# Holding TensorE's products to the order in which the program emits them

## The chip, the cores and the metric

The kernel runs on one core of a Trainium2 chip. The metric is the device time of one execution in microseconds (us), lower is better. A run's figure is the median of several executions.

## The reference

A block of four sequence mixers over 2048 tokens of 1024 features, depth 1, all in fp32:

```python
h = _rmsnorm(x, pre_norm_w)
proj = einsum('btd,de->bte', h, w_in)          # 1024 -> 3984 columns
p_gdn, p_rwkv, p_sc, p_gla = _split(proj, [1032, 1152, 1024, 784])
y = concatenate([_gated_deltanet(p_gdn), _rwkv7(p_rwkv), _short_conv(p_sc), _gla(p_gla)])
out = einsum('bte,ed->btd', y, w_out)
x = x + _rmsnorm(out, post_norm_w)
```

Gated DeltaNet, RWKV-7 and GLA are recurrences over time with 4 heads each. The kernel computes them in chunks of 64 tokens: inside a chunk with small matrix products, and for the first two with the inverse of a triangular 64x64 matrix; from chunk to chunk a state is carried. The short convolution has no state beyond two tokens.

## The kernel before, in words

**The large products.** Time is cut into four blocks of 512 tokens. For each block the input projection is computed in 31 tiles of 128 columns and one narrow tile (called "x" in the code). An fp32 product is made of three fp32r products (high times high, high times low, low times high), so that a tile takes 24 products of 128x128 by 512, in groups of 4: 760 of them in a block (method `proj`, line 476). They accumulate in the PSUM tile `pp`, of which there are two. The output projection (`out_proj`, line 1345) has the same form: 16 time tiles by 48 products.

**The small products.** All else on TensorE is small: transposes (`psa`, by `tr`), chunk matrices (`psa<-AR,BK`, `psa<-kq`), the inverses (`inverse`, line 558: twelve steps, each a handful of products into `psi` followed by VectorE work on the result) and the chains that carry the states (`psc`: `gdn_chain`, `rwkv_chain`, `gla`). Each step of an inverse or a chain needs the step before it, through VectorE or ScalarE.

**The order of emission.** Every kind of work is a Python generator, a "thread" with a priority: the chains 0, the inverses 1, the preparation of matrices 2, output of finished tiles 3, statistics and the scaled input of the next block 4, loading of the output weights 5, and 99 for the main thread, the projections. `weave` (line 227) decides what is emitted next by a clock of its own, `self.t`, that `mm` and `tr` advance by an estimate of each product's time (a group of four large products counts 0.86 us). The main thread emits one group at a time. When at least `BEAT = 2.3` us of that clock have gone by since the last visit, that is after three groups or 12 large products, and some other thread is ready, all ready threads are stepped until none is ready: a visit. A thread that yields a number is ready again that much later; the numbers stand in the table `LAT` (0.48 to 8 us). A thread that yields a tuple waits until that event has been declared by `done`, plus its `lat`. If the main thread itself waits for an event, the visits follow each other with no large products between them, and the clock jumps ahead where nobody is ready.

Three such waits of the main thread matter here:

- `projections` (line 1394) puts ("R", blk - 1) before the first RWKV tile of a block (line 1404), because the tiles that hold the last block's RWKV operands are used again. The event comes from `put` (line 1196): 8.0 us after the last RWKV chain step of the last block its result is transposed (`psa<-cst,or`, two products a time tile), and 3.0 us after that ("R", blk - 1) holds (line 1203).
- `proj` waits for "F", pieces of the scaled input of the next block (`hh` and `hl`, method `front`, line 405).
- `out_proj` begins with `yield "W", 0` (line 1347). `load_out` (line 1333) starts to load the output weights when ("G", 3) holds, 3.0 us after the last DeltaNet transposes (`psa<-cst,og`), and steps eight times with 2.8 us (`LAT["wo0"]`); the event comes 2.0 us later.

**The compiled order.** The program is then scheduled at compile time. The scheduler takes each engine's instructions in the order of emission as long as they are ready by its own model of times; where the next one isn't, it lets a later one that is ready go first, on TensorE as on the others. Some instructions stand in `high_priority` blocks and go ahead; no product is among them. TensorE then runs its products in the compiled order, and waits where one's input is late.

Of the kernel before, what the change touches and what calls it, by code (L numbers as in the profile page):

```python
# [125 lines left out]
class Ring:  # L126


    def __init__(self, pool, name, shape, dtype, n):
        self.t = [pool.tile(shape, dtype, name=f"{name}{i}", tag=f"{name}{i}") for i in range(n)]  # L130
        self.i = 0
# [56 lines left out]
class K:  # L188
    def __init__(self, tc, a, out):
        self.tc, self.nc, self.a, self.out = tc, tc.nc, a, out  # L190
        self.t, self.left, self.ev, self.threads = 0.0, 0.0, {}, []


    def mm(self, out, w, x, **kw):
        n = math.prod(out.shape[1:])
        self.t += max(0.028, n * (1.67e-3 if w.dtype == F32 else 0.42e-3))
        return self.nc.tensor.matmul(out, w, x, **kw)  # L197

    def tr(self, out, x, ident):
        self.t += out.shape[1] * 0.83e-3  # L200
        return self.nc.tensor.transpose(out, x, ident)  # L201

    def thread(self, gen, prio):
        self.threads.append([prio, 0.0, None, gen])
# [1253 lines left out]
```

## Time and profile before

| what | value |
|---|---|
| median of three runs | 1382.74 us (1379.66 to 1382.91) |
| the profiled execution | 1378.93 us |
| its span in the trace | 1377.1 us |
| mean granted TensorE clock | 0.986 |
| TensorE (PE) busy | 1287.9 us, 94% |
| VectorE (DVE) busy | 973.3 us, 71% |
| ScalarE (ACT), GpSimd (POOL) busy | 530.4 us, 360.3 us |

The span is the time from the first to the last instruction in the trace; 1.8 us of the execution lie around it. All durations below are from this one execution. PE rows in the trace have modelled ends, so the time a group of products takes is best read as the distance from its start to the start of what follows it on PE. An fp32 product stands as two rows of the hardware (x16 is eight products in the code); fp32r, fp16 products and transposes stand as one.

### The profile page before, as it was taken

The numbers are of one execution on the slowest core, as the hardware profiler recorded it, in microseconds if no ns is written. First come the engines' busy times: TensorE is split into PE (matmuls) and PEld (weight loads), VectorE is DVE, ScalarE is ACT, GpSimd is POOL, SyncE is SP. The second block draws the span as 40 slices with busy tenths as digits, with TensorE's granted clock in tenths as the row PEclk, the third lists the DMA queues.
The fourth block names the chain that finished last, engine by engine and source line by source line (L and its number), as shares of the span: only waits on it lengthen the run. The fifth ranks groups of instructions, "written<-read, shape, count | busy, mean of one in ns | idle before, by whom it ended". The sixth has DMA issues, their size and how long they took to land. (4 is left out here: it accounts for less than half of the span.)

```text
span 1377.1 us, 25663 instructions
## 1 busy us (share of the span) xinstructions
PE 1287.9 (94%) x9928; PEld 978.6 (71%) x9928; DVE 973.3 (71%) x2194; ACT 530.4 (39%) x1181; POOL 360.3 (26%) x437
## 2 busy tenths in 40 slices
PE   5979987899999999999999899999999998999997
PEld 3767765677777767777677677676776775677886
DVE  4767489989874897687847985878659948744322
ACT  4654345344532341335423523353225325232221
POOL 5555454311121121111301210103112126223221
PEclk9999999999999999999999999999999998999999
DMA  7876653444344324554344344442443344333442
GB/s 262 281 257 218 238 179 127 156 135 141 127 134 151 126 99 150 159 156 136 124 152 136 104 140 160 144 134 72 140 159 112 129 143 138 102 100 119 151 148 100
DMA packets 98507, 204.48 MB, mean 148 GB/s; under 512 B 9152, under 2 KB 39248, under 8 KB 98384
## 3 DMA queue, kind: packets, MB, share of 16 engines
q1 hardware_dynamic: 98384, 202.83, 44.9%
q8 instruction: 78, 1.28, 0.4%
q14 instruction: 45, 0.37, 0.1%
HBM read 153.51 MB, written 49.28 MB: 147 GB/s over the span
## 5 line engine op out<-in xcount | busy, mean ns | idle before, releaser
L197 PE MATMUL pp<-hh,w 128*128 128x512 f32 (+1 forms) x2272 | 646.6, 407 | 8.7 <-ACT hh L432 5.2
L197 PEld LDWEIGHTS pp<-hh,w 128*128 128x128 f32 (+1 forms) x2272 | 415.0, 190 | 99.9 <-ACT hh L432 4.8
L197 PE MATMUL pp<-hl,w 128*128 128x512 f32 (+1 forms) x1152 | 339.5, 405 | 2.2 <-POOL hl L433 2.0
L197 PEld LDWEIGHTS pp<-hl,w 128*128 128x128 f32 (+1 forms) x1152 | 208.2, 188 | 48.4 <-POOL hl L433 3.8
L350 POOL TENSOR_TENSOR w<-raw,w 128x512 fp32r<-128x512 f32 (+1 forms) x102 | 131.2, 1288 | 212.8 <-ACT w L349 120.1
L349 ACT CAST w<-raw 128x512 fp32r<-128x512 f32 (+1 forms) x102 | 60.3, 593 | 146.4 <-PE pp L197 74.8
L354 POOL TENSOR_TENSOR sm<-sm,mhalf 128x4 f32<-128x4 f32 (+1 forms) x64 | 58.6, 915 | 213.0 <-DVE sm L1091 185.5
L197 PE MATMUL pp<-woh,w 128*128 128x512 f32 x256 | 73.2, 402 | 1.1 <-ACT w L349 1.1
L659 DVE SCALAR_TENSOR_TENSOR pq<-pq,par,pq 128x512 f32<-128x512 f32 x72 | 58.9, 817 | 15.3 <-ACT pq L656 10.4
L583 DVE COPY Yb<-Y 64x512 f16<-64x512 f16 x160 | 63.5, 397 | 1.8
L833 ACT COPY pq<-pp 128x512 f32<-128x512 f32 x36 | 21.1, 587 | 97.7 <-PE pp L197 97.7
L197 PEld LDWEIGHTS pp<-woh,w 128*128 128x128 f32 x256 | 47.5, 190 | 10.7 <-ACT w L349 1.5
L1030 DVE TENSOR_TENSOR Sg<-Sg,psc 64x128 f32<-64x128 f32 x64 | 18.1, 283 | 46.9 <-PE psc L197 46.1
L596 DVE TENSOR_TENSOR X<-psi,X 128x512 f16<-128x512 f32 x64 | 43.9, 686 | 8.7 <-PE psi L197 8.2
L197 PEld LDWEIGHTS <-Bb 128*128 128x128 f16 x768 | 29.7, 99 | 28.5 <-issue 19.9
L197 PEld LDWEIGHTS <-Yb 128*128 128x128 f16 x640 | 25.4, 99 | 33.5 <-issue 23.3
L197 PE MATMUL psi<-X,Bb 128*128 128x64 f16 x768 | 39.3, 195 | 9.7 <-DVE X L579 7.0
L197 PE MATMUL psi<-W,Yb 128*128 128x64 f16 x640 | 33.0, 195 | 15.5 <-DVE W L591 12.7
L1391 DVE SCALAR_TENSOR_TENSOR pq<-pq,sm,x 128x512 f32<-128x512 f32 x32 | 24.5, 765 | 30.3 <-DMA x<-in_x 20.4
L598 DVE STREAM_TRANSPOSE Y<-X 128x512 f16<-128x512 f16 x64 | 45.1, 704 | 0.5
L591 DVE TENSOR_TENSOR W<-psi,c 128x512 f16<-128x512 f32 x64 | 43.8, 685 | 2.0 <-PE psi L197 0.7
L1380 ACT ACTIVATE x<-pp 128x512 f32<-128x512 f32 x32 | 19.1, 597 | 55.8 <-PE pp L197 55.8
(317 smaller groups left out, 2101.1 us busy)
## 6 DMA issues: line engine op xcount, KB each, us to landing
w<-parts SPq DMA_DIRECT2D x186, 512.0 KB, 3.3
parts<-w SPq DMA_DIRECT2D x62, 512.0 KB, 4.0
raw<-in_wt SPq DMA_DIRECT2D x62, 256.0 KB, 3.1
x<-in_x SPq DMA_DIRECT2D x56, 256.0 KB, 3.0
raw<-yd SPq DMA_DIRECT2D x32, 256.0 KB, 2.9
out<-pq SPq DMA_DIRECT2D x32, 256.0 KB, 2.1
x<-in_xt SPq DMA_DIRECT2D x24, 256.0 KB, 2.7
yd<-y SPq DMA_DIRECT2D x48, 128.0 KB, 1.8
```

Source lines behind the costliest of these rows:

```text
L197: return self.nc.tensor.matmul(out, w, x, **kw)
L349: self.nc.scalar.copy(hi, src)
L350: self.nc.gpsimd.tensor_tensor(lo, src, hi.bitcast(F32), ALU.subtract)
L354: self.nc.gpsimd.tensor_tensor(dst, x, self.mhalf[:, 0:x.shape[1]], ALU.pow)
L583: nc.vector.tensor_copy(Yb[hs(c), :, hs(c)], Y[hs(c)])
L591: nc.vector.tensor_tensor(W, v(ps), m4(self.lev[lv]), ALU.mult)
L596: nc.vector.tensor_tensor(X2, v(ps), X, ALU.add)
L598: nc.vector.transpose(Y, X)
L659: nc.vector.scalar_tensor_tensor(acc, p[:, i:i + BL], self.pcol("conv", 4 * ct + i), acc, ALU.mult, ALU.add)
L833: nc.scalar.copy(p[:, 1:], ps)
L1380: nc.scalar.activation(junk, ps[i], AF.Square, accum_out=ss[:, i:i + 1])
L1391: nc.vector.scalar_tensor_tensor(o, o, r, x, ALU.mult, ALU.add)
```

## The change

Every product and transpose is given an order-only dependency on the one emitted before it. The scheduler thus has to keep TensorE's instructions in the order of emission. No semaphore comes with it; nothing else is edited, `BEAT` and `LAT` included. The orders of the other engines are still the scheduler's.

```diff
     def mm(self, out, w, x, **kw):
         n = math.prod(out.shape[1:])
         self.t += max(0.028, n * (1.67e-3 if w.dtype == F32 else 0.42e-3))
-        return self.nc.tensor.matmul(out, w, x, **kw)
+        return self.after(self.nc.tensor.matmul(out, w, x, **kw))
 
     def tr(self, out, x, ident):
         self.t += out.shape[1] * 0.83e-3
-        return self.nc.tensor.transpose(out, x, ident)
+        return self.after(self.nc.tensor.transpose(out, x, ident))
+
+    def after(self, ins):
+
+        if self.prev is not None:
+            info = mybir.DependencyInfo(mybir.DependencyClass.NoSync, mybir.DependencyReason.DATA)
+            self.tc.add_manual_dep(ins.ins, self.prev.ins.name, info, reason="order of emission")
+        self.prev = ins
+        return ins
```

## Rows read from the trace of the kernel before

**Rows 1.** The page, part 1: busy us (share of the span) xinstructions.
```profile
PE 1287.9 (94%) x9928; PEld 978.6 (71%) x9928; DVE 973.3 (71%) x2194; ACT 530.4 (39%) x1181; POOL 360.3 (26%) x437
```
**Rows 2.** Busy time by stretch; columns: stretch, its us, PE, PEld, DVE, ACT, POOL, clock, DMA.
```profile
418.84:704.82 285.98, 274.81 (x2296) 207.49 (x2291) 219.26 (x520) 111.27 (x254) 48.29 (x74) 0.99 0.43 138
...
684.80:728.00 43.20, 43.20 (x342) 33.75 (x341) 21.27 (x48) 11.51 (x25) 4.29 (x13) 1.00 0.49 156
757.50:806.70 49.20, 44.27 (x344) 33.40 (x342) 46.50 (x99) 21.67 (x48) 10.86 (x10) 0.97 0.32 105
847.90:888.00 40.10, 36.56 (x294) 26.74 (x294) 34.87 (x79) 17.25 (x39) 6.63 (x10) 1.00 0.48 153
...
645.65:664.80 19.15, 18.56 (x169) 12.28 (x167) 16.11 (x56) 11.72 (x33) 6.05 (x8) 1.00 0.51 159
```
**Rows 3.** Timeline of PE, an undisturbed stretch; columns: start, us, instruction.
```profile
684.77 1.17 PE L197 MATMUL pp<-hh,w 128*128 128x512 f32 x4
685.78 1.08 PE L197 MATMUL pp<-hl,w 128*128 128x512 f32 x4
686.70 1.08 PE L197 MATMUL pp<-hh,w 128*128 128x512 f32 x4
687.71 0.65 PE L197 MATMUL psa<-qbd,lqk 128*64 128x256 f32 x4
```
**Rows 4.** Timeline 645 to 670 us, first RWKV tile of block 2: PE, DVE, ACT.
```profile
645.65 1.19 PE L197 MATMUL pp<-hh,w 128*128 128x512 f32 x4
...
652.10 0.73 PE L197 MATMUL pp<-hh,w 128*128 128x512 f32 x2
652.67 0.27 PE L201 MATMUL psa<-cst,lg 128*128 128x128 f32 x1
...
659.68 0.42 DVE L1095 TENSOR_TENSOR or<-or,sm 128x256 f32<-128x256 f32 x1 [0.90 <-POOL sm L354]
...
662.11 0.59 ACT L833 COPY pq<-pp 128x512 f32<-128x512 f32 x1
...
663.45 1.05 PE L197 MATMUL pp<-hh,w 128*128 128x512 f32 x3
...
664.80 0.44 PE L201 MATMUL psa<-cst,or 128*128 128x128 f32 x2
...
669.94 0.39 PE L197 MATMUL psi<-X,Bb 128*128 128x64 f16 x8 [1.96 <-DVE X L579]
```
**Rows 5.** Timeline 757 to 807 us, preparation of RWKV matrices in block 2.
```profile
757.52 1.18 PE L197 MATMUL pp<-hh,w 128*128 128x512 f32 x4
...
763.59 0.39 PE L197 MATMUL psi<-W,Yb 128*128 128x64 f16 x8 [1.94 <-DVE W L591]
...
805.48 0.70 PE L197 MATMUL pp<-hh,w 128*128 128x512 f32 x2
```
**Rows 6.** Timeline: last DeltaNet transposes, and the output projection's first products.
```profile
1129.85 0.44 PE L201 MATMUL psa<-cst,og 128*128 128x128 f32 x2
...
1149.20 1.22 PE L197 MATMUL pp<-woh,w 128*128 128x512 f32 x2 [1.09 <-ACT w L349]
...
1153.98 0.66 PE L201 MATMUL psa<-cst,or 128*128 128x128 f32 x2
...
1157.14 0.52 PE L197 MATMUL pp<-woh,w 128*128 128x512 f32 x1
```
**Rows 7.** Busy time by stretch around it, columns as in rows 2.
```profile
1140.20:1147.00 6.80, 4.46 (x76) 3.85 (x76) 5.22 (x10) 5.47 (x14) 4.73 (x4) 1.00 0.51 146
1147.00:1157.20 10.20, 7.69 (x29) 4.73 (x29) 9.33 (x18) 5.56 (x14) 6.51 (x6) 0.50 0.44 125
```
**Rows 8.** Timeline of PE at the start: the first large products.
```profile
14.71 1.94 PE L197 MATMUL pp<-hh,w 128*64 128x512 f32 x4 [1.58 <-ACT hh L432]
16.45 2.13 PE L197 MATMUL pp<-hl,w 128*64 128x512 f32 x4
```

## How the change should move the time

> **What bounds the kernel.** I read the engines' busy time first: TensorE is busy 94% of the span, VectorE 71% [rows 1], so TensorE is the bound and only 89 us of it are idle. Then the busy time by stretch [rows 2]. One period of the program (418.84 to 704.82) has 11 us of TensorE idle time. In 684.8 to 728 TensorE has no gap at all; the gaps lie where VectorE is nearly full (757.5 to 806.7: 46.50 of 49.20 us) or where it and the chains are (847.9 to 888.0). Then the timeline of TensorE against the rule of emission. In the undisturbed stretch the large products come in twelves, as `weave` emits them [rows 3]: three groups, 0.92 us apart, 0.23 us a product, and 0.18 us more for the change between kinds (2.94 us in all). There the compiled order already is that of emission and the change does nothing. Elsewhere the twelves are broken: in 757.5 to 806.7 the timeline has 108 large products in 21 pieces instead of 9 (from the first to the last row of [rows 5]), and in 645.65 to 664.80 28 products in 11 pieces [rows 4]. A piece costs about 0.12 us beside its products (two products took 0.57 us from 652.10 to 652.67, against 0.46). These places are what the change edits, and the question is what each held place waits for.
>
> **The change, part by part.** It adds no instruction and no semaphore; on TensorE a product that isn't ready now holds back all that was emitted behind it.
>
> *First RWKV tile of a block, three times (blocks 1 to 3).* The code lets the main thread emit this tile only after ("R", blk - 1), that is after the last transposes `psa<-cst,or` of the block before. In the trace the tile's 24 products start at 645.65 and are evicted at 662.11, and 28 large products are done before those transposes run at 664.80 [rows 4]. The scheduler pulled all of them forward, into the waits of RWKV's and GLA's chains. Held, nothing large is there to fill in. Worked out: the transposes' input is ready at 660.10 (659.68 + 0.42), so they run 4.7 us earlier than before; behind them come the 28 products, 28 x 0.23 = 6.4 us and 0.4 us for three visits. Net 6.8 - 4.7 = +2.1 us. The event comes 3.0 us of the emission's clock later still, so some steps of the chain and the inverse run bare; the nearest row is the step at 669.94 that waits 1.96 us, and I take half of one more such wait, +1.0. The clock: after the one place where TensorE ran small products alone (1140.2 to 1147.0, busy 4.46 of 6.80 us) the granted clock was 0.50, 1.2 GHz, for the next 10.2 us [rows 7], whereas 645.65 to 664.80 kept 1.00 [rows 2]. Held, this stretch becomes like the other. I let the first eight large products run at half clock: four took 1.74 us at the start, 0.435 each [rows 8], 0.2 more than 0.23, +1.6. Fewer pieces in what follows give back some six changes, -0.7. Together +4.0, three times +12. Bounds for each: -1 (chain steps come sooner by what TensorE's large products delay them now, and the clock stays), +9 (6.8 us not covered at all, a full wait of 1.96 and no gain of pieces).
>
> By the Trainium skill, page "TensorE: Matmul & The Clock Gate", section "Part 4: PE-mode transpose", transposes do not count as activity for the clock in the way products do. With it the held stretches, rich in transposes, would run at the lower clock throughout, which is the second rival below.
>
> *Start of the output projection, once.* The main thread waits for "W", 0. The last DeltaNet transposes ran at 1129.85 [rows 6]; the event is 3.0 + 8 x 2.8 + 2.0 = 27.4 us later on the emission's clock, which while the main thread waits I take to run like real time: 1157.3. Before, the first product ran at 1149.20, and nine had run by 1157.3 (counted from 1149.20 to 1157.14 [rows 6]), at half clock [rows 7]. Held, nine products move behind, 9 x 0.23 = 2.1 us, and eight of those after the wait meet the half clock, +1.6; at the density of [rows 4], eight changes saved in 19.15 us, the next 35 us save 15, -1.7 (an estimate). Sum +2. Bounds -2 (chains and inverse, alone on TensorE, finish sooner) and +8.1 (1157.3 - 1149.2).
>
> *Preparation of RWKV matrices, four times (757.5 to 806.7).* The inverse's step at 763.59 was passed by five products more than the twelve, and still waited 1.94 us for VectorE [rows 5]. Held, TensorE waits 5 x 0.23 = 1.15 us longer there, but the products come after, while VectorE, which is busy 46.50 of 49.20 us and keeps its work, sets the pace. Twelve pieces fewer are worth 1.4 us. I take +0.5 each, +2. Bounds each: -2.7 (VectorE without a gap) and, taking the same 2.7 us once more as lost, +2.7.
>
> *The next block's first tile, three times (847.9 to 888.0).* TensorE waits 3.5 us there now, VectorE is busy 34.87 of 40.10. The tile waits for the same `hh` in either order; and pieces saved and chain steps held back behind it are of like size. 0, bounds -2 and +2 each.
>
> *Start.* The first tile's products, now taken as the pieces of `hh` come (14.71 on, at half clock), stand in pairs in the emission; one product waits for its neighbour, +0.5 [rows 8].
>
> The other engines' orders are set by priorities that the edit leaves alone: the waits that it adds delay evictions of `pp` and so the next tiles' products, both counted above as products moved. Loads of weights move with their products and are waited for nowhere in these rows except at 1149.20.
>
> Sum: 12 + 2 + 2 + 0 + 0.5 = +16.5 us on the profiled execution's 1378.93 us: 1395.4. The runs shown lie 1 to 4 us above that execution (median 1382.74), so I say **1397 us**, about 1% slower. What can be told from no change here is 0.3%, 4 us.
>
> **Rivals.** *Faster: the emission knows better than the scheduler.* The table of latencies is in the kernel's own terms, and where it fits the chip, held products wait no longer than now and the pieces vanish. Price: 8 changes saved in 645.65 to 664.80, 12 in 757.5 to 806.7 and as many in 847.9 to 888.0 (an estimate from the former), 32 x 0.12 = 3.8 us a block, 15 us in four; time about 1366. It decides if each RWKV wait costs less than 4 us, what a block saves. For it: TensorE gaps of only 11 us a block would remain even so. Against it: the three waits above are in the code, and the trace shows 28 products that passed each. Chance 0.20.
>
> *Much slower: the held stretches lose the clock.* In the three RWKV stretches TensorE is granted half its clock throughout, like 1147.0 to 1157.2. There the two transposes took 0.66 us against 0.44 [rows 4, 6]; the 12 us of small products of such a stretch (18.56 busy less 6.4) become 18: +6 each, +18 in all, 1415. For it: [rows 7]. Against: those products wait on VectorE half the time anyway. Chance 0.17.
>
> *Nothing to tell.* The products that move behind the transposes merely take the place of the pieces and of the waits that are there now: within 4 us of 1382.7. Chance 0.13. *The change does not do what it says*, because the scheduler's order is the emission's nearly everywhere or the dependency is not honoured: the same time, 0.05; against it, [rows 4] shows an order that cannot stay.
>
> **How the numbers follow.** My forecast has 0.45; its own range is 1387 (where slower begins) to 1408 (the RWKV waits at +8 each, near their bound). With the half clock 0.17 and it, slower by over 0.3% has 0.62; the same 0.18; faster 0.20. The range takes in most of each neighbour: low 1374 (half of the faster case's gain, and the low bounds of the terms), high 1420 (the half clock and a little more).
>
> **What would show it.** In the profile after, no large product between the visit at about 641 us and the last `psa<-cst,or` of the block, and a gap-rich stretch there in each of three blocks, with the granted clock at 0.50 in or after it. Twelves nearly everywhere else. TensorE's idle time up from 89 us by 15 or more, its busy time the same or less by the pieces. The first `pp<-woh` near 1157 plus the delay so far. It is wrong if those stretches are no longer than now, if large products still stand in them, or if TensorE's idle time grows in 757.5 to 806.7 rather than there.

## The result, and where the time went

The changed kernel takes 1474.92 us (median of four runs, 1473.68 to 1476.17), the kernel before 1381.64 us beside it: a ratio of 1.0677, 95% interval 1.0658 to 1.0695. The forecast was 1397 us with 1420 as its upper end: the sign was right, the size wrong by a factor of about six.

The first view is the page of the changed kernel: its span, TensorE's busy line (that of before is [rows 1]), and the granted clock of forty slices in tenths of full speed.

```profile
span 1471.9 us, 25671 instructions
...
PE 1310.6 (89%) x9928; PEld 1015.7 (69%) x9928; DVE 966.2 (66%) x2194; ACT 530.5 (36%) x1181; POOL 353.9 (24%) x437
...
PEclk9999988889799989998899899996999897799999
```

The same instructions leave TensorE idle for 1471.9 - 1310.6 = 161 us; before it was 1377.1 - 1287.9 = 89 us. That is +72 us of idle time, and +23 us of busy time, which make the +94.8 us of the two spans. The busy time grew although every product is the same, and the clock fell more often: the mean granted clock is 0.926 against 0.986. At two levels, 1 and 0.5, that means about 2 x 0.074 x 1471.9 = 218 us at 1.2 GHz, against 2 x 0.014 x 1377.1 = 39 us.

Where both came from is seen by laying the two traces side by side. The order of the small products is nearly the same in both, so a stretch can be cut at the same two small products. The next view is the changed kernel's busy time in six stretches: the four bare ones around a block's end (the first in block 0, the others the three RWKV waits), one preparation of RWKV matrices, and the start of the output projection. Columns as in [rows 2].

```profile
282.05:310.13 28.08, 18.14 (x236) 14.64 (x235) 20.25 (x51) 8.36 (x21) 2.26 (x3) 0.61 0.15 51
377.50:408.38 30.88, 23.75 (x285) 16.79 (x285) 23.36 (x78) 14.29 (x41) 8.24 (x11) 0.72 0.31 95
684.43:716.33 31.90, 22.92 (x285) 16.45 (x285) 24.97 (x89) 15.07 (x42) 8.47 (x11) 0.75 0.31 92
991.88:1026.18 34.30, 25.47 (x285) 17.41 (x285) 24.84 (x89) 9.53 (x25) 8.46 (x11) 0.65 0.06 20
814.81:862.97 48.16, 41.61 (x329) 33.04 (x328) 40.19 (x92) 18.81 (x44) 7.60 (x9) 0.86 0.26 86
1221.56:1255.08 33.52, 15.11 (x201) 12.68 (x201) 28.84 (x59) 15.91 (x37) 21.85 (x19) 0.66 0.42 128
```

And the same small products in the kernel before:

```profile
276.15:301.51 25.36, 24.91 (x280) 18.04 (x280) 21.46 (x53) 10.82 (x26) 1.84 (x3) 1.00 0.47 146
357.33:385.19 27.86, 26.51 (x313) 18.39 (x314) 23.10 (x78) 15.40 (x44) 8.58 (x12) 1.00 0.46 141
641.36:673.11 31.75, 28.76 (x322) 19.94 (x322) 27.89 (x91) 17.66 (x47) 11.83 (x15) 1.00 0.40 124
928.09:960.18 32.09, 30.13 (x324) 20.43 (x323) 26.88 (x91) 13.16 (x33) 11.50 (x15) 1.00 0.18 59
763.59:806.69 43.10, 40.11 (x323) 30.19 (x323) 40.50 (x89) 19.39 (x45) 8.48 (x9) 0.96 0.29 96
1140.17:1173.84 33.67, 26.18 (x246) 18.86 (x246) 30.25 (x57) 17.79 (x41) 22.26 (x20) 0.85 0.48 134
```

This pair is the main reading of the case. Large products are counted here from a stretch's first small product to its last, and the ends of the stretches are cut to within 0.4 us. Take the third line of each. In block 2, 31.75 us before and 31.90 us after: the same length. But the stretch before holds 35 large products beside the small ones (TensorE busy 28.76 us at full clock), and that after holds none (22.92 us at 0.75). The chains set the length either way, and the large products inside cost next to nothing. Held, the 35 still have to run, behind the stretch, at their full price. The output projection's line says the same: 33.67 us with 40 large products, 33.52 with none. The first stretch and the RWKV waits of blocks 1 and 3 held 44, 27 and 36 before and none after, and bare they are even longer, by 2.7, 3.0 and 2.2 us, at clocks of 0.61, 0.72 and 0.65. From the start of the third stretch to the point where the same large products are done, it took 43.41 us before (641.36 to 684.77) and 51.37 after (684.43 to 735.80): +8.0, which is 35 x 0.23. The preparation of the RWKV matrices (fifth line) differs: it has 91 large products before and 96 after, and it grew from 43.10 to 48.16 us.

The timeline of TensorE in the changed kernel, start of the third stretch, shows what sets the length. Columns as in [rows 3], in brackets the idle time before.

```profile
684.43 0.45 PE L197 MATMUL psc<-UV,BK 128*64 128x64 f32 x8
684.71 0.64 PE L197 MATMUL psc<-UV,M 128*64 128x64 f32 x16
686.17 0.68 PE L197 MATMUL psc<-UV,M 64*64 64x64 f32 x16 [0.83 <-DVE Sr L1038]
686.79 0.71 PE L197 MATMUL psc<-Sr,AR 128*128 128x128 f32 x4
687.95 0.45 PE L197 MATMUL psc<-ru,Yf 64*64 64x64 f32 x8 [0.46 <-ACT ru L1057]
689.39 0.45 PE L197 MATMUL psc<-UV,BK 128*64 128x64 f32 x8 [0.99 <-DVE UV L1065]
692.03 1.23 PE L197 MATMUL psc<-Sr,AR 128*128 128x128 f32 x4 [2.18 <-DVE Sr L1038]
...
709.86 0.44 PE L201 MATMUL psa<-cst,or 128*128 128x128 f32 x2 [0.53 <-ACT t L792]
...
716.33 1.56 PE L197 MATMUL pp<-hh,w 128*128 128x512 f32 x4
```

Most chain steps wait for VectorE or ScalarE. Four rows of `psc<-Sr,AR` stand at 0.71 us before the wait of 2.18 us and at 1.23 after it: the granted clock is 1.00 from 684.43 to 689.90 and 0.50 from there to 703.50. The last transposes `psa<-cst,or` stand 25.4 us after the stretch's start (709.86 - 684.43); before, with all those large products in the way, it was 23.4 (664.80 [rows 4] - 641.36).

The releasers with the most TensorE waits in the changed kernel: changed kernel first, then the kernel before (the same statements, eight lines higher); columns: total us, times, longest.

```profile
PE psi L197 <- DVE W L599: 26.6, 13, 5.2
PE psc L197 <- DVE UV L1065: 20.7, 16, 3.5
PE psc L197 <- DVE gu L1007: 15.3, 6, 3.7
PE psc L197 <- DVE Sr L1038: 14.9, 9, 4.7
```
```profile
PE psi L197 <- DVE W L591: 12.7, 8, 4.3
...
PE psc L197 <- DVE UV L1057: 3.5, 5, 1.3
...
PE psc L197 <- DVE gu L999: 2.1, 5, 1.1
...
PE psc L197 <- DVE Sr L1030: 0.7, 3, 0.3
```

Four links of the chains and the inverse have 77.5 us of waits where they had 19.0: 58 of the 72 us.

### The profile page after: what moved, and what is told of

The parts are those of the page before. It is cut to its first block, busy times and chain, and to the rows that moved or that the text cites. A ratio compares the mean times of both kernels' runs of the same rounds, so it can differ in the third digit from the quotient of the medians.

```text
span 1471.9 us, 25671 instructions
## 1 busy us (share of the span) xinstructions
PE 1310.6 (89%) x9928; PEld 1015.7 (69%) x9928; DVE 966.2 (66%) x2194; ACT 530.5 (36%) x1181; POOL 353.9 (24%) x437
## 4 chain that ended last, share of the span: by engine, by line
PE 56%; DVE 17%; issue 3%; ACT 3%; POOL 2%; DMA 2%; ACTq 0%; POOLq 0%; DVEq 0%
PE pp L197 41%; PE psc L197 7%; PE psi L197 3%; PE psa L197 3%; PE psa L201 2%; POOL sm L362 1%; DVE Y L606 1%; DVE Yb L591 1%; DVE X L604 1%; DVE pq L667 1%; DMA w<-parts 1%; DVE M L957 1%; DVE UV L1065 1%; DVE W L599 1%; DVE t L887 0%
## 5 line engine op out<-in xcount | busy, mean ns | idle before, releaser
L197 PEld LDWEIGHTS pp<-hh,w 128*128 128x128 f32 (+1 forms) x2272 | 426.6, 194 | 97.9 <-DMA w<-parts 4.5
L197 PEld LDWEIGHTS pp<-hl,w 128*128 128x128 f32 (+1 forms) x1152 | 219.4, 195 | 53.4 <-issue 3.6
L667 DVE SCALAR_TENSOR_TENSOR pq<-pq,par,pq 128x512 f32<-128x512 f32 x72 | 58.7, 815 | 21.5 <-ACT pq L664 16.6
L197 PEld LDWEIGHTS <-Yb 128*128 128x128 f16 x640 | 27.5, 103 | 50.2 <-issue 31.5
L591 DVE COPY Yb<-Y 64x512 f16<-64x512 f16 x160 | 58.2, 364 | 2.0
L197 PEld LDWEIGHTS <-Bb 128*128 128x128 f16 x768 | 30.9, 101 | 24.9 <-issue 21.3
```

What stands on the lines that cost most here:

```text
L197: return self.after(self.nc.tensor.matmul(out, w, x, **kw))
L591: nc.vector.tensor_copy(Yb[hs(c), :, hs(c)], Y[hs(c)])
L667: nc.vector.scalar_tensor_tensor(acc, p[:, i:i + BL], self.pcol("conv", 4 * ct + i), acc, ALU.mult, ALU.add)
```

## The experiments

The theory after the result (theory 1, later A, "cover"): what is lost is the large work that used to lie inside waits of small chains. Against it stood that the held order of the small products is itself bad (theory 2), later that freed work only moves the hole (B), and that the half clock is the price (C).

In all edits below but those of the clock at the end, `mm` is told which products are large, and `after` keeps two memories: `prev`, the last product that others wait for, and `prevL`, the last large one.

```diff
-    def after(self, ins):
+    def after(self, ins, free=None):
+        behind = [self.prevL] if free else [self.prev] if free is None else [self.prev, self.prevL]
+        for p in behind:
...
+        if free is not None:
+            self.prevL = ins
+        if not free:
+            self.prev = ins
```

`free=True` is a large product that need not wait for small ones, `free=False` a large one held as in the change, and `None` a small one.

**Two chains.** All large products free, so that large and small are each held among themselves.

```diff
-                    self.mm(ps[0:w.shape[2]], w[:, k, :], h[:, 4 * i + k, :], start=(i + q + k == 0),
+                    self.mm(ps[0:w.shape[2]], w[:, k, :], h[:, 4 * i + k, :], free=True, start=(i + q + k == 0),
```

> The change with the hold split in two: the large products of both projections keep their order among themselves, the small ones theirs, and neither waits for the other. Theory 1 (the loss is that nothing large may fill the small products' waits): the time goes back to that of the kernel before, 1380 to 1390 us. Theory 2 (the small products' own order of emission is at fault, late ones holding back small ones behind them): at least half of the loss stays, above 1425 us.

Measured: 1379.28 us, ratio 0.9959 (0.9936 to 0.9982). The whole loss is gone, and the order of the small products is still held. So that order costs nothing; only the large products' place does. Its stretches of block 2 and 3 (the second view's third and fourth line):

```profile
642.09:674.02 31.93, 28.72 (x329) 20.24 (x329) 25.98 (x91) 17.52 (x47) 11.57 (x15) 1.00 0.47 140
928.51:959.98 31.47, 29.06 (x332) 20.91 (x332) 25.94 (x91) 12.83 (x31) 11.40 (x15) 1.00 0.23 75
```

With 42 and 45 large products inside, the lengths are still 31.9 and 31.5 us, and the clock is 1.00.

**Only the first RWKV tile of a block free**, the output projection free, and both. The conditions are `free=tiles[j][0] == WT_RWKV + 8` in `proj` and `free=True` in `out_proj`.

> The change, but the 24 products of the first RWKV tile of a block may go ahead of small products emitted before them. Theory 1 (the three stretches in which the main thread waits for the last block's RWKV result cost 8 to 13 us each, as the two traces compare): 25 to 35 us less than the change, 1440 to 1450 us. My forecast's size of that step (4 us each): about 1463 us.

Measured: 1470.64 us, ratio 1.0621 (1.0573 to 1.0668). A miss: 4 us less than the change by the medians, 8 by the ratios, not 25 to 35. Its trace by stretch:

```profile
681.90:696.27 14.37, 13.38 (x146) 9.28 (x145) 12.56 (x52) 8.35 (x23) 2.46 (x4) 1.00 0.46 148
696.27:714.53 18.26, 14.53 (x165) 9.92 (x164) 12.72 (x40) 9.81 (x26) 9.39 (x12) 0.72 0.32 102
```

The tile's 24 products go into the first 14.37 us and keep the clock at 1.00; the rest, 18.26 us, is bare again (0.72). And the small products of the visits for which those 24 had been emitted now have nothing beside them, since the next tile is held. Behind the stretch two steps of the inverse wait bare:

```profile
715.16 0.39 PE L197 MATMUL psi<-X,Bb 128*128 128x64 f16 x8 [0.78 <-DVE X L608]
717.38 0.41 PE L197 MATMUL psi<-W,Yb 128*128 128x64 f16 x8 [1.82 <-DVE Yb L595]
```

From the stretch's start to the point where the same large products are done it took 50.2 us (681.90 to 732.08), against 51.37 in the changed kernel and 43.41 before.

> The change, but the products of the output projection may go ahead of small products emitted before them. Theory 1: the wait for the output weights costs about 15 us of the last 20 us that the traces differ by, so 1457 to 1463 us. My forecast's size (2 us): about 1473 us.

Measured: 1462.14 us, ratio 1.0568 (1.0509 to 1.0626), about 13 us less by the medians, 15 by the ratios, as expected.

> Both of these at once. Theory 1 with sums: the two gains add up, 1425 to 1435 us, and what is left over the kernel before, 45 to 55 us, belongs to places where the main thread waits for nothing and small products wait for VectorE (5 to 7 us in each of some seven stretches) and to the first block. If the waits of the main thread were all of it: below 1395 us.

Measured: 1459.34 us, ratio 1.0530 (1.0482 to 1.0578): the gains of the two add up within their intervals, and the first tile's is as small as alone; a miss again.

**Whole families of tiles free.** If the hole moves because the neighbours are held, a whole family must do what one tile did not.

```diff
-                    self.mm(ps[0:w.shape[2]], w[:, k, :], h[:, 4 * i + k, :], start=(i + q + k == 0),
+                    self.mm(ps[0:w.shape[2]], w[:, k, :], h[:, 4 * i + k, :], free=tiles[j][0] != 'x' and WT_RWKV <= tiles[j][0] < WT_SC, start=(i + q + k == 0),
```

(For the other two: `WT_SC <= tiles[j][0] < WT_GLA`; and `tiles[j][0] == 'x' or tiles[j][0] < WT_RWKV or tiles[j][0] >= WT_GLA`.)

> Held as in the changed kernel (1474.9 us), but the large products of all nine RWKV tiles (216 of a block's products) may start before small products emitted earlier. In the compiled order they then run up to 38, 42 and 45 products ahead around the three waits for the previous block's RWKV chain, as many as with two separate chains, and 0 ahead everywhere else. Theory A (cover: what a wait costs is the small chain's time that no large product fills, and with the tile family freed the visits behind the wait stay filled too): the three bare stretches of 31 to 34 us go, 25 to 38 us come back, 1437 to 1450. Theory B (the hole moves, as with only the first tile freed, where 4 us came back: products that fill the wait are missing where they were emitted): 4 to 10 us, 1465 to 1471. Theory C (the half clock is the main price, and it follows the number of bare stretches rather than their length): the three stretches' half-clock time of about 60 us goes, worth 10 to 15 us, 1460 to 1465.

> Held as in the changed kernel, but the large products of the short-convolution tiles may start before small products emitted earlier. Theory A (cover): only the stretches that prepare the RWKV matrices (808.70 to 862.97 in the changed kernel, 5 us longer than before) come back, 4 times about 5 us: 1452 to 1460. Theory B (the hole moves): 0 to 8 us, 1467 to 1475.

> Held as in the changed kernel, but the large products of the GLA, decay and GDN tiles may start before small products emitted earlier. Theory A (cover): the stretches around the end of a block (903.76 to 960.12, 6.7 us longer than before, three or four times) and block 1's wait for the GDN chain (about 12 us) come back: 20 to 35 us, 1440 to 1455. Theory B (the hole moves): 4 to 12 us, 1463 to 1471. Together with the RWKV tiles, the short-convolution tiles and the output projection (13 us), theory A wants the four gains to add up to about the 93 us that are gone; theory B wants their sum far below, because only freeing all of them keeps the holes filled.

| freed | us | ratio (interval) | points of the ratio back |
|---|---|---|---|
| RWKV tiles | 1447.28 | 1.0456 (1.0427 to 1.0486) | 2.21 |
| short-convolution tiles | 1457.37 | 1.0540 (1.0504 to 1.0576) | 1.37 |
| GLA, decay, GDN tiles | 1446.37 | 1.0453 (1.0427 to 1.0480) | 2.24 |
| output projection (above) | 1462.14 | 1.0568 (1.0509 to 1.0626) | 1.09 |
| sum | | | 6.91 |
| all (two chains) | 1379.28 | 0.9959 (0.9936 to 0.9982) | 7.18 |

Theory A holds in all three, and the four parts add up to the whole within their intervals. The three RWKV waits with their family free, with 38, 42 and 45 large products in each:

```profile
375.79:409.25 33.46, 29.10 (x323) 20.40 (x324) 25.23 (x81) 17.55 (x48) 11.44 (x16) 0.93 0.43 135
682.35:713.70 31.35, 28.64 (x329) 20.24 (x329) 25.90 (x91) 17.73 (x47) 11.70 (x15) 1.00 0.45 143
979.38:1010.88 31.50, 29.11 (x332) 20.90 (x332) 25.92 (x91) 12.82 (x31) 11.40 (x15) 1.00 0.23 75
```

The last is shorter than the bare one (31.50 against 34.30), the first is longer (33.46 against 30.88); together the three take 96.3 us filled and 97.1 bare. With the short-convolution tiles free, the preparation of the RWKV matrices is back to its old length (43.10 before, 48.16 held):

```profile
812.42:854.85 42.43, 36.32 (x325) 28.00 (x325) 41.23 (x90) 18.79 (x44) 8.29 (x9) 1.00 0.29 97
```

**A sliding lead.** How far ahead must a large product be allowed to go? `was` keeps, for each large product, the last small one that was emitted before it.

```diff
+        if free:
+            self.was.append(self.prev)
+            behind = [self.prevL, self.was[max(0, len(self.was) - 1 - 24)]]
+        else:
+            behind = [self.prev, self.prevL]
```

> Every large product may start before small products emitted earlier, but at most 24 large products ahead of the order of emission (a sliding lead; the changed kernel allows 0, two separate chains reach 52 in block 0, 38 to 45 at the three RWKV waits, 69 in the output projection and 15 elsewhere). Theory A (cover in proportion): all the places that need 15 or less come back whole, those that need 40 to 45 by 24 of 42, the output projection by 24 of 69: about 20 to 28 us of the 93 stay lost, 1400 to 1412. Theory B (the hole moves, a partial lead gives nearly nothing at the long waits): the RWKV waits, the block-0 stretches and the output projection stay lost, 1420 to 1445.

> The sliding lead lowered to 12 large products, one interval between visits. Theory A (cover in proportion): at the long waits 12 of 40 to 45, in the output projection 12 of 69, elsewhere nearly all of the 15 come back: of the 93 us about 45 stay lost, 1420 to 1435. Theory B (threshold: a wait is either covered or not, so that under one full interval a lead gives little): 1445 to 1470.

> The sliding lead raised to 60 large products: in the compiled order it binds nowhere but in the output projection (60 instead of 69). Theory A (cover): nothing is left of the loss, 1374 to 1384, as two separate chains (1379.3, 0.4% under the kernel before). Theory B (holding the small products' own order costs something too): 1386 to 1400.

| lead allowed | us | ratio (interval) |
|---|---|---|
| 0 (the change) | 1474.92 | 1.0677 (1.0658 to 1.0695) |
| 12 | 1427.38 | 1.0310 (1.0271 to 1.0349) |
| 24 | 1412.01 | 1.0206 (1.0176 to 1.0237) |
| 60 | 1381.03 | 0.9981 (0.9962 to 1.0001) |

The gain follows the lead (at 24 the time lies at the upper end of theory A's range); there is no threshold, so theory B falls here too. One interval of twelve gives back half, since most places need no more than 15, and the long waits go on gaining up to 40 and more. In block 2 the RWKV wait is 33.08 us long at a lead of 12 and 32.03 at 24:

```profile
665.59:698.67 33.08, 27.70 (x299) 19.32 (x299) 25.41 (x90) 15.42 (x44) 8.47 (x12) 0.74 0.35 105
```
```profile
657.05:689.08 32.03, 27.23 (x311) 18.57 (x311) 25.04 (x92) 17.58 (x47) 11.42 (x15) 0.89 0.39 121
```

So with 0, 12, 24, 35 and 42 large products inside, the same wait takes 31.90, 33.08, 32.03, 31.75 and 31.93 us. The other places are not all so even. Between the starts of the same two small products, block 1's wait takes 30.8, 30.9, 32.4 and 32.5 us at leads of 0, 12, 24 and 60, block 3's 34.3, 32.5, 32.3 and 31.1. At the output projection, 52 large products stand inside with two chains, and the stretch takes 39.2 us where it takes 33.5 bare: there a product costs 0.11 us and not nothing.

**Two chains, two groups between visits** (`BEAT` from 2.3 to 1.5).

> Two separate chains as in the version at 1379.3, with two groups of large products between visits instead of three (the interval 1.5 us of the program's own clock, not 2.3). Theory A (cover): large products go ahead wherever the small chain waits, so the interval of emission hardly matters: 1373 to 1386. Theory D (the emitted interval itself sets how early the chains are visited): the chains get further on per projection, the waits for them shrink, 1355 to 1370; or the finer pieces of work disturb the large products, 1390 to 1410.

Measured: 1378.77 us, ratio 0.9968 (0.9948 to 0.9989). The interval of emission hardly matters once large products may go ahead. Both forms of two chains are 0.3 to 0.4% faster than the kernel before, by the middle of their intervals, which exclude no change only by 0.1 to 0.2%. The lead of 60, whose order differs from that of two chains by little, has an interval that ends at 1.0001.

**The clock alone.** Work that nobody needs is put into the three RWKV waits of the changed kernel, to hold the clock up without cover.

```diff
+    def fill(self):
+        if self.junk is None:
+            self.junk = self.pp()
+        for _ in range(2):
+            self.after(self.nc.tensor.matmul(self.junk[:, 0:256], self.bones_r, self.up[:, 0, :], start=True, stop=True))
...
                     for th in ready:
                         self.step(th)
+                        if main[0] == 99 and main[2] is not None and main[2][0] == "R" and not self.can(main):
+                            self.fill()
```

> Held as in the changed kernel, and while the projections are blocked at the three waits for the RWKV chain, two products whose result nobody reads (128x256, into a PSUM tile of the projections) are emitted behind each step of a visit, some 60 to 70 at each wait, about 0.11 us each at full clock. They keep TensorE busy and do no work, so they tell the price of the half clock in a bare stretch from the price of the missing cover. Theory A (cover): the small chain's own latency sets the stretch; the clock of the three stretches (now 0.72, 0.75, 0.65) rises, but 7 us of dummies take what the faster clock gives: 1470 to 1482. Theory C (the half clock): the small products, 23 to 25 us of busy time in each stretch at these clocks, run at full speed, each stretch loses 4 to 7 us, 1454 to 1463.

Measured: 1479.86 us, ratio 1.0693 (1.0655 to 1.0731). The three waits, first all engines, then in the second wait the dummy products alone (columns there: PE, PEld, clock, DMA):

```profile
377.88:409.60 31.72, 28.75 (x344) 23.16 (x345) 23.07 (x79) 14.42 (x41) 9.35 (x12) 0.89 0.28 89
688.12:721.77 33.65, 27.32 (x348) 22.01 (x347) 25.48 (x91) 14.61 (x41) 9.79 (x12) 0.95 0.27 83
998.58:1036.79 38.21, 32.45 (x347) 25.95 (x347) 24.82 (x88) 9.35 (x25) 8.81 (x11) 0.78 0.06 19
...
688.12:721.77 33.65, 13.21 (x62) 9.40 (x62) 0.95 0.27 83
```

The clock rose from 0.72, 0.75 and 0.65, and the small products ran faster: their own rows, taken without the dummies, are busy for 20.7, 19.4 and 22.9 us where it was 23.9, 23.1 and 25.6. Yet no stretch became shorter. The next expectation rests on two wrong readings of these lines. The difference of two lines (27.32 - 13.21 = 14.1 in the second wait) was taken for the small products' busy time, a fall of 8 us; but the modelled ends of the dummies overlap the rows behind them, and the fall is 3 to 4 us. And 13.21 us over 62 dummies was taken for the price of one, 0.21. From start to start, ten of them take 1.38 us at full clock, close to the 0.11 each that the expectation above had put down:

```profile
688.97 1.45 PE L216 MATMUL pp<-up,bones 128*128 128x256 f32 x10
690.35 0.68 PE L198 MATMUL psc<-UV,M 64*64 64x64 f32 x16
```

Beside the small products the dummies add 8 to 10 us of busy time in a wait, about the idle time that there was (7 to 9 us). One dummy a step instead of two (`range(1)`) leaves more room:

> One product that nobody reads behind each step of a visit during the three RWKV waits instead of two: about 31 in a wait, measured at 0.22 us each in the run with two, 7 us of the 7 to 9 us that TensorE idles there in the changed kernel (with two it was 13 to 15 us, more than the idle time, the small products' own busy time fell by 8 us in a wait and the stretches grew by 0.8 to 3.9 us). Theory C (the half clock is a price of its own): with less in the way the faster small products show, each stretch is 3 to 6 us shorter than in the changed kernel, 1456 to 1466. Theory A (cover, the clock only a companion): the stretches stay within 1 us of the changed kernel's 30.9, 31.9 and 34.3, 1471 to 1479. A clock that stays low with 7 us of dummies would leave it open.

Measured: 1479.11 us, ratio 1.0691 (1.0655 to 1.0728). The waits:

```profile
375.31:406.01 30.70, 25.89 (x315) 19.85 (x315) 22.93 (x79) 14.70 (x42) 8.37 (x11) 0.87 0.32 96
685.91:721.02 35.11, 27.88 (x316) 21.12 (x316) 24.71 (x91) 14.67 (x41) 9.43 (x12) 0.81 0.24 80
996.39:1032.32 35.93, 28.56 (x316) 21.64 (x316) 24.47 (x89) 9.54 (x25) 8.47 (x11) 0.76 0.06 19
```

Beside the small products the dummies now add some 5 us in a wait, and the small products are busy for 21.5, 22.5 and 23.2 us. The waits are 30.70, 35.11 and 35.93 us long against 30.9, 31.9 and 34.3: none is shorter by 3 to 6 us. Theory C's forecast failed in both runs: more activity in the waits won nothing back. Theory A's figure was missed on two of the stretches, which are longer by 3.2 and 1.6 us. What stays open is the half clock's exact share: the clock never reached 1.00 in these runs (0.87, 0.81 and 0.76 in the second), and dummies can stand in the chains' way themselves. In block 3's wait some of that share seems to show: bare at 0.65 it takes 34.3 us, filled at 1.00 31.1. A rough bound from above is TensorE's busy time, 1310.6 us against 1274.6 with two chains, so 36 of the 96 us between those two spans.

## Why the prediction was wrong, step by step

- **What bounds the kernel, and where the change acts.** Right: TensorE, and an undisturbed stretch does not change. The stretch [rows 2] gives as 684.80 to 728.00 lies at 735.80 in the changed kernel and runs without a gap (43.20 of 43.20 us), at clock 1.00. The places that were named are among those that lost time, and look as described: no large product from 684.43 to the last `psa<-cst,or` at 709.86, and a granted clock below 1.00. One sign was wrong: TensorE's busy time was to stay or fall, and rose by 23 us.
- **First RWKV tile of a block: the step that failed, and the principle behind it.** "28 x 0.23 = 6.4 us and 0.4 us" were set against "they run 4.7 us earlier than before", so that +2.1 was left. The credit of 4.7 us did not come: the transposes ran 2 us later after the stretch's start (25.4 against 23.4). That is not the lower clock alone, for with the RWKV family free, 42 large products inside and the clock at 1.00, they run 25.8 us after it. Large products had not been in the chain's way; they had lain in its waits. So the price is gross. Nor was 28 the right count. What counts is how many products are ahead at the end of the wait, and that is 35 in block 2. 35 x 0.23 = 8.1, and +8.0 was measured there. Freeing the RWKV family gave back 2.21 points, 30 us or 10 us a wait; the sum had 4.0. Its upper bound of 9 was added up without the 1.6 us of half clock that the term itself has; with them it is 10.4.
- **Preparation of RWKV matrices.** I took "VectorE ... sets the pace" from 46.50 of 49.20 us and priced five passed products at nothing but +0.5. In the changed kernel VectorE is busy as long as before (40.19 and 40.50 us) in a stretch that is 5 us longer, so held it no longer sets the pace but waits itself. With the short-convolution tiles free it is nearly full again (41.23 of 42.43 us). The lead there reaches 15, and 15 x 0.23 = 3.5 with the clock at 0.86 besides. Predicted 4 x 0.5 = 2 us with a bound of 2.7 each; the short-convolution tiles gave back 1.37 points, 19 us.
- **Next block's first tile, priced 0.** The stretch that starts at 847.50 before takes 47.18 us up to the same small product, 53.88 us in the changed kernel: +6.7 and not within 2. With the GLA, decay and GDN tiles free it takes 49.34 us. "Pieces saved and chain steps held back are of like size" was an assertion with no row behind it.
- **A wait overlooked.** Block 1 starts with a wait for ("G", 0). I had looked at the period from 418.84 on, and there the wait is covered. Around block 0's end (282.05 to 310.13) 44 large products had run inside it, some 10 us.
- **Start of the output projection.** Nine products counted; with two chains the lead reaches 69. I let the clock of the emission run like real time while the main thread waits, 27.4 us from the last `psa<-cst,og` to the first `pp<-woh`. In the changed kernel it took 44.0:

```profile
1211.04 0.44 PE L201 MATMUL psa<-cst,og 128*128 128x128 f32 x2
...
1255.08 2.05 PE L197 MATMUL pp<-woh,w 128*128 128x512 f32 x4
```

The emission orders the waits of the inverse and the chains in front of that product, and TensorE waits each of them out. Predicted +2, bound +8.1; 1.09 points, about 15 us, came back.
- **The rivals.** The half clock was a rival for three stretches at 1415 us. It came, in part of each of them (0.72, 0.75, 0.65) and elsewhere, as a companion of missing cover. The Trainium skill, page "TensorE: Matmul & The Clock Gate", section "Part 4: PE-mode transpose", says that transposes do not count as activity for the clock as products do; from it I had a rival with the half clock throughout. Mean clocks of 0.61 to 0.75 are neither 0.50 nor 1.00, and no run here separates transposes from products. Nor were the held stretches "rich in transposes": of block 2's 284 small products 14 are transposes (line 201), 3.4 of 22.9 us.
- **The pieces.** The faster rival lived on 0.12 us a broken twelve. The large products stand in 418 pieces before and in 268 after. So 150 pieces were saved, some 18 us at that price, in a kernel that lost 93 us: large products in the waits outweigh them. What a piece is really worth, no run shows; two chains have 369.

A sum with the gross price would have been close. Leads at the waits (large products done ahead of the order of emission, the largest at each place, counted with two chains or with one family free): 38 + 42 + 45 (RWKV), 8 + 15 + 15 + 15 (preparation), 11 + 52 + 8 + 8 (GDN and the blocks' ends), 69 (output): 326 products x 0.23 us = 75 us. The rest of the 93 goes along with the lower clock; no run splits it further.

## What to carry to other kernels

On an engine that is the bound, work pulled forward into the waits of a latency-bound chain was nearly free (38 to 45 products of 0.23 us changed the length of an RWKV wait by -3 to +2 us), and taking it out cost about its full time: count those instructions, and give no credit for the chain unless a row shows it waiting behind them. If an order has to be held on such an engine, hold it within each kind of work and leave the kinds free against each other; here that took back all of a 6.8% loss. Look at the first period and the last as well as at the steady one, since the largest leads stood there (52 and 69 products).

## What was not expected of the hardware

A stretch of 284 small products kept its length within some 4% (31.75 to 33.08 us) whether 0, 12, 24, 35 or 42 products of 128x128 by 512 lay in it, while its mean clock lay between 0.74 and 1.00. And busy time overstates what a single product takes from the others: 62 dummy products (128x256) stand as 13.21 us, 0.21 each, yet ten in a row took 1.38 us from start to start at full clock, 0.14 each, where one of 512 columns takes 0.23 [rows 3].
